# A state-space layer and an MLP on one core: table sums moved between GpSimd, VectorE and TensorE

## The chip, the core and the metric

The kernel runs on one core of a Trainium2 chip. The core has TensorE (PE, matmuls, with its weight loads as PEld), VectorE (DVE), ScalarE (ACT), GpSimd (POOL) and SyncE (SP, which issues the DMAs here). Each runs its own instructions in a fixed order, and they wait for one another by semaphores. The metric is the device time of one execution in microseconds (us), as the median of several runs. Times inside an execution come from one profiled execution, counted from the start of its span.

## What is computed

One layer of a diffusion backbone over 256 latent and 256 context tokens of width 2048: an S5 state-space mixer, a GLU, and a squared-ReLU MLP, each with RMSNorm and modulation by a conditioning vector.

```python
h = modulate(rmsnorm(x, norm_mix_pre), sh1, sc1)        # ctx and latent, own shift and scale
lam_bar = exp(lam * dt); b_bar = ((lam_bar - 1) / lam)[..., None] * b   # 128 groups, 64 states, complex
for direction in range(2):                               # forward and reverse
    st_ctx = s5_scan(u_ctx, lam_bar, b_bar, 0)           # s[t] = lam_bar * s[t-1] + b_bar u[t]
    st_lat = s5_scan(u_lat, lam_bar, b_bar, st_ctx_final)
    y = y + einsum('btgp,ghp->btgh', st_lat, c_mat).real
a, g = split(gelu(y) @ w_glu); y = a * sigmoid(g)
x = x + gt1 * rmsnorm(y, norm_mix_post)
x = x + gt2 * rmsnorm(square(relu(modulate(rmsnorm(x, norm_mlp_pre), sh2, sc2) @ w1)) @ w2, norm_mlp_post)
```

## The kernel before

The 256 time steps are cut into 32 chunks of 8, and the 128 groups into 16 blocks of 8 groups, each block into two half blocks of 4 groups. All of the S5 mixer lies in about the first 420 us.

**Per half block, the input tables (E).** A chunk's input reaches the state through b_bar times powers of lam_bar. The product of two complex numbers is made with three multiplications. GpSimd makes the sums s1e = Qr + Qi (Q are the powers) and s2e = Br + Bi, Br - Bi (`e_sums`, once a block). VectorE makes the three products k = s1e*Br, Qr*s2e, Qi*s2e (`e_op`, 128x512 each), then subtracts the latter two from k into e[1] and e[0] (two more 128x512 instructions, e<-k,e in the profile). PE transposes the eight 128x128 parts of e against the identity (`e_tr`, tile tr), ScalarE copies them to et (`e_ev`). PE also multiplies e with the diagonal blocks cbd of C into a "strip" st (`strip`), from which the table for the within-chunk part comes, over wps and W, and a DMA round trip through DRAM (wd, then eight DMAs into it). With et and the normalised input xz, PE makes the chunk inputs (`v_mm`, tile v), which ScalarE copies (`v_ev`) into the tables ctx and lat.

**Per unit of 4, 6 and 6 blocks, the scan.** VectorE runs over the context chunks in a tree of steps and over the latent chunks one by one, 31 steps of three instructions each (lines 727, 732 and 734, tiles t, ctx, lat), which depend on each other.

**Per block, the output.** `d_sums` on GpSimd makes s1d and s2d from the powers P and from C (loaded as bcc); VectorE makes three products for each half block (`d_op`, tiles dx in a ring of 4 buffers, dy for the last two blocks). ScalarE copies the states out of lat (`sp_copy`, two instructions), GpSimd adds their real and imaginary parts (`sp_sum`), and PE makes y (`out_mm`), followed by Gelu.

Beside this PE multiplies the conditioning vector with its weights (tile ada, from loads raw<-wa and raw<-wk of 1 MB each into three buffers), and GpSimd applies norm and modulation to the input (xz<-xz,rs and xz<-xz,vec). Behind S5 come the GLU (tile gb, PE) and the MLP (tiles m and o, PE), which the change does not touch.

What sets the order: `Plan` takes every task with its engine, an assumed duration, what it depends on, and rings of buffers that it takes and gives back, and lists them engine by engine; each engine then runs its list in that order, whatever the real times. SP's list holds all loads. A table `PR` holds priorities and where the sums run (`sums`, `spsum`). In the profile, line 122 is the helper for all tensor_tensor instructions, and line 125 that for ScalarE's activations, so there one goes by tiles.

Of the kernel before, what the change touches and what calls it, by code (L numbers as in the profile page):

```python
# [116 lines left out]
def _body(ctx, tc, nc, I, O):  # L117
# [111 lines left out]
    with psx:  # L229
# [55 lines left out]
        sk = ew.tile([128, L, 4, H], F32, name="sk")  # L285
        cbd = [ew.tile([128, 8, 2, 32], F32, name=f"cbd{n}") for n in range(2)]
# [116 lines left out]
        for name, cap in (("ada", 1), ("ev", 1), ("bcb", 2), ("bcs", 2), ("bcc", 2), ("s1e", 2), ("s2e", 1), ("sd", 2), ("cbd", 2),  # L403
                          ("k1", 1), ("dd", 1), ("e", 2), ("et", 2), ("tr", 2), ("st", 1), ("v", 1), ("x", 2), ("yv", 1), ("sk", 1), ("W", 1), ("it", 1),
                          ("ctx", 1), ("lat", 2), ("dx", 4), ("sp", 2), ("z", 1), ("t", 1), ("it2", 1)):
            plan.ring(name, [0.0] * cap)
# [7 lines left out]
        PR = dict(ada=4, T=20, st=3, V=1, W=5, om=5, E=0, D=2, D0=8, gate=0, k4=5, gap=1, p=-1, ars=3, g=6, g2=20, evm=10, eg1=6, x1=6, zlo=4, z=8, ada2=0, k4l=4, acc=20, lo=1, hi=5, sums='Pool', spsum='Pool')  # L414
# [35 lines left out]
        pt = [add("ACT", 0.95, lambda d=d, s=s, g=g, l=l: p_copy(d, s, g, l), prio=PR["p"]) for d, s, g in ((Pr, pr, 1.0), (Pn, pi, -1.0)) for l in (True, False)]  # L450
        t = []
# [179 lines left out]
        def strip(b, hf):  # L631
            e = est[b, hf][1]
# [75 lines left out]
        def v_ev(b, hf):  # L708
# [7 lines left out]
            act(cx[:, :, :, gu:gu + 4], pv[:, 0:32])  # L716
            act(lt[:, 1:, :, gu:gu + 4], pv[:, 32:63])
# [41 lines left out]
        def d_op(b, hf, f):  # L759
# [51 lines left out]
        for b in range(NB):  # L811
# [4 lines left out]
            esum = add(PR["sums"], 0.55 if on_v else 1.1, lambda b=b: e_sums(b), ([bcl["b", b]] if b > 1 else []) + gate + (qt if b == 2 else []), prio=1, take=("s1e", "s2e"))  # L816
            cb = add("ACT", 0.6, lambda b=b: c_diag(b), [bcl["s", b]] if b > 1 else [], prio=1, take=("cbd",), give=("bcs",))
            for hf in range(2):
                p = PR["E"]
                o = [add("DVE", 0.6, lambda b=b, h=hf: e_op(b, h, 0), [esum], prio=p, take=("k1", "e"))]  # L820
                for k in (1, 2):
                    o.append(add("DVE", 0.6, lambda b=b, h=hf, k=k: e_op(b, h, k), [(o[-1], 0.0)], prio=p))
                o.append(add("DVE", 0.6, lambda b=b, h=hf: e_op(b, h, 3), [(o[0], 0.13), (o[2], 0.13)], prio=p))
                o.append(add("DVE", 0.6, lambda b=b, h=hf: e_op(b, h, 4), [(o[3], 0.0), (o[1], 0.13)], prio=p, give=("k1",) + (("s1e", "s2e", "bcb") if hf else ())))
                tps, evs = [], []
                for r in range(2):
                    tps.append(add("PE", 0.43, lambda b=b, h=hf, r=r: e_tr(b, h, r), [o[3 + r]] + tps, prio=PR["T"], take=("tr",)))
                    evs.append(add("ACT", 0.48, lambda b=b, h=hf, r=r: e_ev(b, h, r), [tps[r]] + [(x, 0.0) for x in evs], prio=0,
                                   take=("et",) if r == 0 else (), give=("tr",)))
                sm = add("PE", 0.57, lambda b=b, h=hf: strip(b, h), [o[4], cb] + tps, prio=PR["st"], take=("st",), give=("e",) + (("cbd",) if hf else ()))  # L830
# [650 lines left out]
```

## Time and profile before

| | before |
|---|---|
| median of 3 runs | 1312.68 us (1308.35 to 1317.29) |
| profiled execution | 1313.43 us, span 1311.7 us |
| PE busy | 1178.7 us (90%) |
| VectorE busy | 897.1 us (68%) |
| ScalarE busy | 539.4 us (41%) |
| GpSimd busy | 192.5 us (15%) |
| granted TensorE clock, mean | 0.953 |
| HBM traffic | 225 GB/s over the span |

The shares of the span are means over stages with different limits, so they are read stretch by stretch. Busy time is the union of an engine's instructions; on PE, matmuls overlap. The granted clock is the share of TensorE's full speed that it was allowed in a stretch. The DMA share is the mean busy share of the core's 16 DMA engines.

### The profile page before, as it was taken

The numbers are of one execution on the slowest core, as the hardware profiler recorded it, in microseconds if no ns is written. First come the engines' busy times: TensorE is split into PE (matmuls) and PEld (weight loads), VectorE is DVE, ScalarE is ACT, GpSimd is POOL, SyncE is SP. The second block draws the span as 40 slices with busy tenths as digits, with TensorE's granted clock in tenths as the row PEclk, the third lists the DMA queues.
The fourth block names the chain that finished last, engine by engine and source line by source line (L and its number), as shares of the span: only waits on it lengthen the run. The fifth ranks groups of instructions, "written<-read, shape, count | busy, mean of one in ns | idle before, by whom it ended". The sixth has DMA issues, their size and how long they took to land.

```text
span 1311.7 us, 22524 instructions
## 1 busy us (share of the span) xinstructions
PE 1178.7 (90%) x9457; PEld 957.2 (73%) x9457; DVE 897.1 (68%) x1200; ACT 539.4 (41%) x731; POOL 192.5 (15%) x200
## 2 busy tenths in 40 slices
PE   4576884696898999989999999999999999999997
PEld 1454553452434688989999999999978888888885
DVE  8999999878878677765555565555655555655555
ACT  5442544242115534574333334333434444444443
POOL 4766344611322000030000000000000000000000
PEclk8588997798899999999999999999999999999998
DMA  7488868989986888816656666566656555555552
GB/s 269 148 213 295 316 245 195 307 307 196 260 227 168 319 346 324 317 66 224 234 219 245 217 220 250 209 242 223 230 189 224 192 193 184 182 185 188 192 192 97
DMA packets 74093, 296.68 MB, mean 226 GB/s; under 512 B 7164, under 2 KB 30588, under 8 KB 48520
## 3 DMA queue, kind: packets, MB, share of 16 engines
q1 hardware_dynamic: 73992, 295.25, 66.3%
q8 instruction: 74, 1.21, 0.4%
q14 instruction: 27, 0.22, 0.1%
HBM read 291.15 MB, written 4.07 MB: 225 GB/s over the span
## 4 chain that ended last, share of the span: by engine, by line
PE 74%; DMA 9%; DVE 5%; SPq 1%; ACT 1%; issue 1%; POOL 0%; DVEq 0%; POOLq 0%; ACTq 0%
PE m L1325 27%; PE o L1358 27%; PE gb L998 9%; DMA raw<-wk 4%; PE gb L991 3%; DMA it<-wd 2%; DMA raw<-wa 2%; DVE e L122 2%; SPq L689 1%; PE ada L484 1%; PE y L800 1%; PE v L706 1%; DMA bcc<-bc 1%; PE m L1247 1%; PE ada L476 1%
## 5 line engine op out<-in xcount | busy, mean ns | idle before, releaser
L122 DVE TENSOR_TENSOR wlo<-raw,whi 128x2048 fp32r<-128x2048 f32 x126 | 288.7, 2291 | 134.7 <-ACT whi L125 134.7
L1325 PE MATMUL m<-h,whi 128*128 128x256 f32 x1984 | 248.2, 283 | 0.0
L125 ACT ACTIVATE whi<-raw 128x2048 fp32r<-128x2048 f32 (+1 forms) x130 | 243.8, 1876 | 1.5 <-PE m L1247 1.5
L1325 PEld LDWEIGHTS m<-h,whi 128*128 128x128 f32 x1984 | 242.5, 192 | 0.0
L1358 PE MATMUL o<-wlo,hh 128*128 128x512 f32 x512 | 160.5, 395 | 0.2 <-DVE wlo L122 0.2
L1358 PE MATMUL o<-whi,hh 128*128 128x512 f32 x512 | 160.6, 395 | 0.0
L1358 PE MATMUL o<-whi,hl 128*128 128x512 f32 x512 | 160.5, 395 | 0.0
L1325 PE MATMUL m<-h,wlo 128*128 128x256 f32 x992 | 129.1, 283 | 0.0
L1325 PEld LDWEIGHTS m<-h,wlo 128*128 128x128 f32 x992 | 123.5, 192 | 0.0
L125 ACT ACTIVATE hh<-hid 128x512 fp32r<-128x512 f32 x64 | 40.5, 633 | 194.5 <-PE o L1358 194.5
L125 ACT ACTIVATE r<-m 128x256 f32<-128x256 f32 x64 | 24.6, 384 | 222.9 <-PE m L1325 221.1
L1358 PEld LDWEIGHTS o<-wlo,hh 128*128 128x128 f32 x512 | 95.9, 187 | 24.1 <-DVE wlo L122 0.6
L1358 PEld LDWEIGHTS o<-whi,hh 128*128 128x128 f32 x512 | 95.8, 187 | 24.2 <-ACT hh L125 0.8
L1358 PEld LDWEIGHTS o<-whi,hl 128*128 128x128 f32 x512 | 96.0, 187 | 23.5
L1297 DVE TENSOR_TENSOR hl<-hid,hh 128x512 fp32r<-128x512 f32 x64 | 44.3, 693 | 88.8 <-ACT hh L125 88.7
L1269 DVE TENSOR_TENSOR hid<-r,m 128x256 f32<-128x256 f32 x64 | 26.9, 421 | 91.9 <-ACT r L125 91.9
L991 PE MATMUL gb<-raw,xz 128*128 128x512 f32 x160 | 76.0, 623 | 2.4 <-DMA raw<-wg 2.3
L623 PE MATMUL tr<-ident,e 128*128 128x128 f32 x256 | 44.7, 315 | 30.9 <-DVE e L122 24.6
L998 PE MATMUL gb<-hi,zs 128*128 128x512 f32 (+1 forms) x288 | 70.1, 357 | 0.0
L484 PE MATMUL ada<-raw,cst 128*32 128x512 f32 x256 | 36.9, 654 | 35.4 <-DMA raw<-wk 35.4
L623 PEld LDWEIGHTS tr<-ident,e 128*128 128x128 f32 x256 | 32.5, 160 | 45.8 <-DVE e L122 21.4
L991 PEld LDWEIGHTS gb<-raw,xz 128*128 128x128 f32 x160 | 30.2, 197 | 46.5 <-issue 40.2
(202 smaller groups left out, 1613.2 us busy)
## 6 DMA issues: line engine op xcount, KB each, us to landing
raw<-w SPq DMA_DIRECT2D x128, 1024.0 KB, 4.8
raw<-wk SPq DMA_DIRECT2D x48, 1024.0 KB, 8.4
raw<-wa SPq DMA_DIRECT2D x32, 1024.0 KB, 7.4
raw<-wg SPq DMA_DIRECT2D x32, 1024.0 KB, 5.2
k<-wk SPq DMA_DIRECT2D x16, 1024.0 KB, 7.3
it<-wd SPq DMA_DIRECT2D x64, 128.0 KB, 6.9
xz<-xs SPq DMA_DIRECT2D x4, 1024.0 KB, 9.1
bcb<-bc SPq DMA_DIRECT2D x16, 128.0 KB, 8.9
```

The costliest lines, as they stand in the source:

```text
L122: eng.tensor_tensor(out=out, in0=a, in1=b, op=op)
L125: A.activation(out=out, in_=in_, func=f, **kw)
L476: PE.matmul(adab["a"][32 * j:32 * j + 32, :n], cst[:, 2 * kt:2 * kt + 32], w[:, e, j], start=(kt == 0), stop=(kt == KT - 1))
L484: PE.matmul(adab["k"][32 * j:32 * j + 32, :], cst[:, 2 * kt:2 * kt + 32], w[:, j * 512:(j + 1) * 512], start=(kt == k0), stop=(kt == KT - ...
L623: PE.transpose(est["ps"][:, gi * 128:(gi + 1) * 128], e[:, r, gi].rearrange("p s h -> p (s h)"), ident)
L689: S.dma_start(it[16 * s:16 * s + 16], wdt[b2][:, :, (7 - s) * H:(7 - s) * H + 128])
L991: PE.matmul(banks[p][nk * t + k], xz[kt // BQ][:, GQ * C + (kt % BQ) * T + t * 128:][:, :128], wt[:, (nk * e + k) * 512:(nk * e + k + 1) * ...
L998: PE.matmul(banks[p][nk * t + k][:, :wd], a, w[:, (nk * e + k) * wd:(nk * e + k + 1) * wd], start=ff, stop=ll)
L1269: V.tensor_tensor(out=hid[:, nt], in0=r, in1=ps, op=ALU.mult)
L1297: V.tensor_tensor(out=hl, in0=hid[:, 2 * i:2 * i + 2], in1=hh.bitcast(F32), op=ALU.subtract)
L1325: PE.matmul(ps, w[a][:, kt], (h2h, h2l)[b][:, kt], start=a == b == kt == 0, stop=a == 1 and kt == KT - 1)
L1358: PE.matmul(banks[nh][2 * t + k], w[2 + x][:, e, zz], w[y][:, e * 1024 + k * 512:e * 1024 + k * 512 + 512], start=f and n == 0 and e == es ...
```

## The change

The subtractions leave VectorE. k gets the negative sum Qs = -(Qr + Qi), which is made once for all blocks (`q_sum`), so that each element of the table is minus (k + e). PE adds the two: for each 128x128 part, a transpose of k starts the sum in PSUM and a transpose of e accumulates on it. The strip's matmuls take k and e one after the other as well. The minus sign is taken out in ScalarE's copies behind PE (scale -1.0). All small sums (s2e, s1d, s2d, sp) now run on VectorE. The ring of k goes from 1 to 2 buffers, that of dx from 4 to 3, and s1e is gone. Since the tasks and their assumed durations change, the planner orders the first 420 us anew.

```diff
+        def q_sum(b0, b1):
+            a, b, o = (w[:, b0:b1].rearrange("p b t g -> p (b t g)") for w in (Qr, Qi, Qs))
+            V.scalar_tensor_tensor(out=o, in0=a, scalar=-1.0, in1=b, op0=ALU.mult, op1=ALU.subtract)
+        q_sum(0, 2)
...
-                          ("k1", 1), ("dd", 1), ("e", 2), ("et", 2), ("tr", 2), ("st", 1), ("v", 1), ("x", 2), ("yv", 1), ("sk", 1), ("W", 1), ("it", 1),
-                          ("ctx", 1), ("lat", 2), ("dx", 4), ("sp", 2), ("z", 1), ("t", 1), ("it2", 1)):
+                          ("k1", 2), ("dd", 1), ("e", 2), ("et", 2), ("tr", 2), ("st", 1), ("v", 1), ("x", 2), ("yv", 1), ("sk", 1), ("W", 1), ("it", 1),
+                          ("ctx", 1), ("lat", 2), ("dx", 3), ("sp", 2), ("z", 1), ("t", 1), ("it2", 1)):
...
-        PR = dict(ada=4, T=20, ..., sums='Pool', spsum='Pool')
+        PR = dict(ada=4, T=20, ..., sums='DVE', spsum='DVE')
...
+        qs = add("DVE", 1.05, lambda: q_sum(2, NB), qt, prio=0)
...
         def e_sums(b):
             Bv = bct.pop(("b", b))
-            s1 = ew.tile([128, L, 8], F32, tag="s1e", bufs=2, name="s1e")
-            tt(SE, s1, Qr[:, b], Qi[:, b], ALU.add)
...
         def e_op(b, hf, k):
-            if k < 3:
-                o, p, c = ((k1, s1, Bv[:, 0]), (e[:, 1], Qr[:, b], s2[:, 0]), (e[:, 0], Qi[:, b], s2[:, 1]))[k]
-                tt(V, o, p[...]..., c[...]..., ALU.mult)
-            else:
-                tt(V, e[:, k - 3], k1, e[:, k - 3], ALU.subtract)
+            o, p, c = ((k1, Qs[:, b], Bv[:, 0]), (e[:, 0], Qi[:, b], s2[:, 1]), (e[:, 1], Qr[:, b], s2[:, 0]))[k]
+            tt(V, o, p[...]..., c[...]..., ALU.mult)
...
             for gi in range(4):
-                PE.transpose(est["ps"][:, gi * 128:(gi + 1) * 128], e[:, r, gi].rearrange("p s h -> p (s h)"), ident)
+                for n, w in enumerate((k1[:, gi], e[:, r, gi])):
+                    PE.matmul(est["ps"][:, gi * 128:(gi + 1) * 128], w.rearrange("p s h -> p (s h)"), ident, is_transpose=True, start=(n == 0), stop=(n == 1))
...
-            for r in range(2):
+            for n, (r, w) in enumerate(((0, k1), (1, k1), (0, e[:, 0]), (1, e[:, 1]))):
                 for j in range(4):
-                    PE.matmul(st[32 * j:32 * j + 32, :128], cbd[b % 2][:, hf * 4 + j, r], e[:, r, j].rearrange("p s h -> p (s h)"),
-                              start=(r == 0), stop=(r == 1))
+                    PE.matmul(st[32 * j:32 * j + 32, :128], cbd[b % 2][:, hf * 4 + j, r], w[:, j].rearrange("p s h -> p (s h)"),
+                              start=(n == 0), stop=(n == 3))
...
-            act(sk[:, :, lp], est.pop(("st", b, hf))[:, :128].rearrange("p (s h) -> p s h", h=H))
+            act(sk[:, :, lp], est.pop(("st", b, hf))[:, :128].rearrange("p (s h) -> p s h", h=H), scale=-1.0)
...
-            act(cx[:, :, :, gu:gu + 4], pv[:, 0:32])
-            act(lt[:, 1:, :, gu:gu + 4], pv[:, 32:63])
+            act(cx[:, :, :, gu:gu + 4], pv[:, 0:32], scale=-1.0)
+            act(lt[:, 1:, :, gu:gu + 4], pv[:, 32:63], scale=-1.0)
```

The order on VectorE, first in the first unit's latent scan (t and lat are the scan's), before:

```order
L122 TENSOR_TENSOR k_1509<-s1e,bcb 128x512
L732 TENSOR_TENSOR lat<-lat,t 128x64
L122 TENSOR_TENSOR e<-Qr,s2e 128x512
L734 TENSOR_TENSOR lat<-lat,t 128x64
L122 TENSOR_TENSOR e<-Qi,s2e 128x512
L727 TENSOR_TENSOR t<-ARS,lat 128x128
L122 TENSOR_TENSOR e<-k_1509,e 128x512
L732 TENSOR_TENSOR lat<-lat,t 128x64
L122 TENSOR_TENSOR e<-k_1509,e 128x512
L734 TENSOR_TENSOR lat<-lat,t 128x64
```

and with the change, in the same scan:

```order
L122 TENSOR_TENSOR k_1955<-Qs,bcb 128x512
L738 TENSOR_TENSOR lat<-lat,t 128x64
L122 TENSOR_TENSOR e<-Qi,s2e 128x512
L740 TENSOR_TENSOR lat<-lat,t 128x64
L122 TENSOR_TENSOR e<-Qr,s2e 128x512
L733 TENSOR_TENSOR t<-ARS,lat 128x128
L518 TENSOR_TENSOR r_2002<-vp,m_65 128x32 x4
L738 TENSOR_TENSOR lat<-lat,t 128x64
L122 TENSOR_TENSOR s2e<-bcb 128x128 x2
```

A half block's five VectorE instructions become three, and the next block's two s2e sums stand among them, which read bcb, a load.

On PE the work of one half block (cbd_146 is the buffer of C's diagonal blocks), before:

```order
L623 MATMUL tr<-ident,e 128x128 x8
L636 MATMUL st<-e,cbd_146 32x128 x8
L706 MATMUL v<-xz_75,et 64x64 x16
L649 MATMUL wps<-ident,sk 64x128 x8
L476 MATMUL ada<-raw,cst 32x256 x8
```

and with the change (the last two pairs of the half block's eight, and what follows):

```order
L629 MATMUL tr<-ident,k_1682 128x128
L629 MATMUL tr<-ident,e 128x128
L629 MATMUL tr<-ident,k_1682 128x128
L629 MATMUL tr<-ident,e 128x128
L642 MATMUL st<-k_1682,cbd_146 32x128 x8
L642 MATMUL st<-e,cbd_146 32x128 x8
L485 MATMUL ada<-raw,cst 32x256 x8
L712 MATMUL v<-xz_76,et 64x64 x16
```

Eight transposes become sixteen, in pairs of k and e, and the strip's eight matmuls become sixteen; v stays.

On VectorE behind the last unit's scan, with the change (before, the rows behind the last lat are the dx products alone, and the sp sums stand on GpSimd):

```order
L740 TENSOR_TENSOR lat<-lat,t 128x96
L122 TENSOR_TENSOR sp<-sp 128x256 x2
L122 TENSOR_TENSOR dx<-s1d,bcc 128x512
L122 TENSOR_TENSOR dx<-Pn,s2d 128x512
L122 TENSOR_TENSOR dx<-Pr,s2d 128x512
L122 TENSOR_TENSOR sp<-sp 128x256
L122 TENSOR_TENSOR dx<-s1d,bcc 128x512
L122 TENSOR_TENSOR dx<-Pn,s2d 128x512
L122 TENSOR_TENSOR dx<-Pr,s2d 128x512
L122 TENSOR_TENSOR s1d<-Pr,Pn 128x64
L122 TENSOR_TENSOR s2d<-bcc 128x128 x2
```

The sums that stood on GpSimd now stand between the products, in VectorE's one order.

## Rows read from the trace of the kernel before

**Rows 1.** Busy time by stretch: stretch, its length, engines, granted clock, DMA share, GB/s.

```profile
20.00:205.00 185.00, 124.80 (x2073) 88.26 (x2077) 176.45 (x351) 73.37 (x175) 98.47 (x99) 0.81 0.70 238
205.00:436.00 231.00, 180.40 (x2041) 96.37 (x2033) 189.92 (x409) 80.64 (x131) 70.33 (x66) 0.91 0.89 241
436.00:560.00 124.00, 124.00 (x633) 103.65 (x632) 94.86 (x80) 56.01 (x77) 0.00 (x0) 1.00 0.85 329
...
586.00:1311.00 725.00, 716.83 (x4520) 644.49 (x4518) 403.82 (x292) 295.45 (x270) 0.95 (x1) 1.00 0.57 206
```

**Rows 2.** Chain that ended last, shares by line, 20 to 205, then 205 to 436.

```profile
by line: DMA raw<-wa 12.0%; DVE e L122 10.4%; PE ada L476 5.2%; DVE lat L734 3.6%; PE v L706 3.6%; DVE t L727 3.4%; DVE lat L732 2.8%; PE tr L623 2.6%; issue 2.3%; DVE k L122 2.0%; PE wps L649 1.7%; PE st L636 1.5%; DVE t L730 1.1%; DVE ctx
...
by line: DMA raw<-wk 20.1%; PE gb L991 14.9%; DMA it<-wd 10.8%; SPq L689 7.3%; PE ada L484 6.7%; PE y L800 5.9%; DMA bcc<-bc 5.5%; DMA raw<-wg 3.7%; DVE dy L122 3.3%; PE v L706 2.7%; PE y L798 2.6%; issue 2.5%; ACT sp L125 2.5%; PE tr L623 
```

**Rows 3.** VectorE by form, 20 to 205: busy us, mean ns; idle before, releasers.

```profile
L122 DVE TENSOR_TENSOR e<-k,e 128x512 f32<-128x512 f32 x46 | 35.1, 771 | 0.1
L122 DVE TENSOR_TENSOR e<-Qr,s2e 128x512 f32<-128x512 f32 x24 | 20.1, 838 | 0.8 <-PE st L636 0.8
L122 DVE TENSOR_TENSOR e<-Qi,s2e 128x512 f32<-128x512 f32 x23 | 20.0, 871 | 0.0
L122 DVE TENSOR_TENSOR k<-s1e,bcb 128x512 f32<-128x512 f32 x24 | 18.9, 789 | 1.2 <-POOL s1e L122 1.2
L727 DVE TENSOR_TENSOR t<-ARS,lat 128x128 f32<-128x128 f32 x29 | 13.2, 455 | 0.3
L734 DVE TENSOR_TENSOR lat<-lat,t 128x64 f32<-128x64 f32 x28 | 11.0, 393 | 0.3
L732 DVE TENSOR_TENSOR lat<-lat,t 128x64 f32<-128x64 f32 x29 | 9.3, 319 | 0.2
```

**Rows 4.** VectorE in order of time: start us, us, instruction.

```profile
59.83 0.29 DVE L433 TENSOR_TENSOR sq<-ARS 128x128 f32<-128x128 f32 x1
60.03 0.28 DVE L434 SCALAR_TENSOR_TENSOR ARS<-ARS 128x128 f32<-128x128 f32 x1
...
61.12 0.68 DVE L122 TENSOR_TENSOR e<-Qr,s2e 128x512 f32<-128x512 f32 x1
61.72 0.68 DVE L122 TENSOR_TENSOR e<-Qi,s2e 128x512 f32<-128x512 f32 x1
...
70.12 1.35 DVE L434 SCALAR_TENSOR_TENSOR ARS<-ARS 128x128 f32<-128x128 f32 x1
...
205.67 0.22 DVE L734 TENSOR_TENSOR lat<-lat,t 128x64 f32<-128x64 f32 x1
```

**Rows 5.** GpSimd in order of time, at the same place.

```profile
68.74 2.57 POOL L122 TENSOR_TENSOR xz<-xz,rs 128x512 f32<-128x512 f32 x2
```

**Rows 6.** GpSimd by form, 20 to 205: the norm and modulation of the input.

```profile
L122 POOL TENSOR_TENSOR xz<-xz,vec 128x512 f32<-128x512 f32 x28 | 38.7, 1391 | 29.1 <-DVE vec L522 28.0
L122 POOL TENSOR_TENSOR xz<-xz,rs 128x512 f32<-128x512 f32 x16 | 23.3, 1484 | 1.0 <-DVE rs L398 1.0
```

**Rows 7.** PE in order of time, two places; a strip matmul has two records.

```profile
129.32 1.09 PE L623 MATMUL tr<-ident,e 128*128 128x128 f32 x4 [0.38 <-DVE e L122]
...
169.57 1.09 PE L623 MATMUL tr<-ident,e 128*128 128x128 f32 x8
170.59 0.65 PE L636 MATMUL st<-e,cbd 128*32 128x128 f32 x16
171.05 1.05 PE L476 MATMUL ada<-raw,cst 128*32 128x256 f32 x16
```

**Rows 8.** PE's waits, 20 to 205: total us, times, longest.

```profile
PE sr L395 <- DVE sr L392: 10.4, 1, 10.4
```

**Rows 9.** GpSimd by form, 205 to 436.

```profile
L122 POOL TENSOR_TENSOR s2d<-bcc 128x128 f32<-128x128 f32 x24 | 18.3, 782 | 41.5 <-DMA bcc<-bc 34.3 <-DVE lat L732 7.2
```

**Rows 10.** VectorE by form, 205 to 436.

```profile
L122 DVE TENSOR_TENSOR dx<-s1d,bcc 128x512 f32<-128x512 f32 x24 | 17.6, 734 | 20.1 <-PE y L800 17.3 <-DMA bcc<-bc 2.8
```

**Rows 11.** ScalarE in order of time, behind the last scan.

```profile
387.00 4.42 ACT L125 ACTIVATE sp<-lat 64x512 f32<-64x512 f32 x4 [10.99 <-DVE lat L734]
```

More of the change, by code (lines that the diff above doesn't have):

```diff
@@ L285, in _body @@
         sk = ew.tile([128, L, 4, H], F32, name="sk")
+        Qs = ew.tile([128, NB, L, 8], F32, name="Qs")
         cbd = [ew.tile([128, 8, 2, 32], F32, name=f"cbd{n}") for n in range(2)]
@@ L402, in _body @@
         add = plan.add
-        for name, cap in (("ada", 1), ("ev", 1), ("bcb", 2), ("bcs", 2), ("bcc", 2), ("s1e", 2), ("s2e", 1), ("sd", 2), ("cbd", 2),
-                          ("k1", 1), ("dd", 1), ("e", 2), ("et", 2), ("tr", 2), ("st", 1), ("v", 1), ("x", 2), ("yv", 1), ("sk", 1), ("W", 1), ("it", 1),
-                          ("ctx", 1), ("lat", 2), ("dx", 4), ("sp", 2), ("z", 1), ("t", 1), ("it2", 1)):
+        for name, cap in (("ada", 1), ("ev", 1), ("bcb", 2), ("bcs", 2), ("bcc", 2), ("s2e", 1), ("sd", 2), ("cbd", 2),
+                          ("k1", 2), ("dd", 1), ("e", 2), ("et", 2), ("tr", 2), ("st", 1), ("v", 1), ("x", 2), ("yv", 1), ("sk", 1), ("W", 1), ("it", 1),
+                          ("ctx", 1), ("lat", 2), ("dx", 3), ("sp", 2), ("z", 1), ("t", 1), ("it2", 1)):
             plan.ring(name, [0.0] * cap)
@@ L412, in dve @@
             return (n * 1.04 + 66) / 1e3
-        PR = dict(ada=4, T=20, st=3, V=1, W=5, om=5, E=0, D=2, D0=8, gate=0, k4=5, gap=1, p=-1, ars=3, g=6, g2=20, evm=10, eg1=6, x1=6, zlo=4, z=8, ada2=0, k4l=4, acc=20, lo=1, hi=5, sums='Pool', spsum='Pool')
+        PR = dict(ada=4, T=20, st=3, V=1, W=5, om=5, E=0, D=2, D0=8, gate=0, k4=5, gap=1, p=-1, ars=3, g=6, g2=20, evm=10, eg1=6, x1=6, zlo=4, z=8, ada2=0, k4l=4, acc=20, lo=1, hi=5, sums='DVE', spsum='DVE')
         SE = V if PR["sums"] == "DVE" else GP
@@ L604, in e_op @@
         def e_op(b, hf, k):
-            Bv, s1, s2 = est[b]
+            Bv, s2 = est[b]
             hs = slice(hf * 4, hf * 4 + 4)
@@ L815, in _body @@
             on_v = PR["sums"] == "DVE"
-            esum = add(PR["sums"], 0.55 if on_v else 1.1, lambda b=b: e_sums(b), ([bcl["b", b]] if b > 1 else []) + gate + (qt if b == 2 else []), prio=1, take=("s1e", "s2e"))
+            esum = add(PR["sums"], 0.55 if on_v else 1.1, lambda b=b: e_sums(b), ([bcl["b", b]] if b > 1 else []) + gate + (qt if b == 2 else []), prio=1, take=("s2e",))
             cb = add("ACT", 0.6, lambda b=b: c_diag(b), [bcl["s", b]] if b > 1 else [], prio=1, take=("cbd",), give=("bcs",))
@@ L819, in _body @@
                 p = PR["E"]
[L820 removed]
+                o = [add("DVE", 0.6, lambda b=b, h=hf: e_op(b, h, 0), [esum] + ([qs] if b == 2 else []), prio=p, take=("k1", "e"))]
                 for k in (1, 2):
[L822 to L824 removed]
+                    o.append(add("DVE", 0.6, lambda b=b, h=hf, k=k: e_op(b, h, k), [(o[-1], 0.0)], prio=p, give=("s2e", "bcb") if hf and k == 2 else ()))
                 tps, evs = [], []
                 for r in range(2):
[L827 removed]
+                    tps.append(add("PE", 0.9, lambda b=b, h=hf, r=r: e_tr(b, h, r), [o[1 + r]] + tps, prio=PR["T"], take=("tr",)))
                     evs.append(add("ACT", 0.48, lambda b=b, h=hf, r=r: e_ev(b, h, r), [tps[r]] + [(x, 0.0) for x in evs], prio=0,
                                    take=("et",) if r == 0 else (), give=("tr",)))
[L830 removed]
+                sm = add("PE", 0.8, lambda b=b, h=hf: strip(b, h), [o[2], cb] + tps, prio=PR["st"], take=("st",), give=("k1", "e") + (("cbd",) if hf else ()))
                 lp = 2 * (b % 2) + hf
```

12 lines of the change are left out of this document (6 added, 6 removed).

## The prediction

> **What bounds the kernel now.** I first cut the span into stretches and read each engine's busy time in them [rows 1]. From 436 us on the change touches nothing: PE is busy 124.00 of 124 us in the GLU and 716.83 of 725 us in the MLP, and these stretches move earlier or later as a block. All edits lie before 436 us, and there two stretches differ. In 20 to 205 us, where 24 of the 32 half blocks build their tables, VectorE is busy 176.45 of 185 us and PE 124.80. In 205 to 436 us VectorE is busy 189.92 of 231, PE 180.40, and the DMA share is 0.89. Second, the chain of the work that ended last, for each stretch [rows 2]: up to 205 us it mixes VectorE's e and scan instructions, PE and the raw loads; behind 205 us it is mostly transfers and their queue: raw<-wk 20.1%, it<-wd 10.8%, SP's issues 7.3%, bcc<-bc 5.5%, raw<-wg 3.7%, together 47%. So VectorE time can be turned into kernel time mainly ahead of 205 us. Third, VectorE's instructions by form [rows 3], and what stands beside the slow ones on GpSimd [rows 4, 5].
>
> **VectorE, 20 to 205 us.** Removed: the subtractions k minus e, 46 in this stretch with a mean of 771 ns [rows 3]. A record is about 0.08 us longer than the step to the next instruction (two 128x512 instructions start at 61.12 and 61.72 us, each of 0.68 us [rows 4]), so each costs 0.69 us: 46 x 0.69 = 31.8 us.
> Added: the 24 s2e sums of 128x128. No such sum ran on VectorE; the nearest row is the 128x128 square at 59.83, whose follower starts at 60.03 [rows 4]: 0.20 us. With eight s2d sums of the same size and four s1d sums of half of it at most that price, 36 x 0.20 = 7.2 us. The new table Qs is one instruction of 128 and one of 896 columns; from 0.20 us at 128 and 0.60 at 512 columns the second is 1.0 us: 1.2 us. Sum 8.4 us.
> Moved off GpSimd: its instructions slow VectorE's. The same ARS instruction (L434) takes 0.28 us at 60.03 and 1.35 us at 70.12, where GpSimd works on xz [rows 4, 5]. Against what such instructions take alone (0.68 us at 512 columns, 0.29 at 128, 0.22 at 64 [rows 4]), the means of [rows 3] hold an excess of 46 x 0.091 + 24 x 0.158 + 23 x 0.191 + 24 x 0.109 + 29 x 0.165 + 28 x 0.173 + 29 x 0.099 = 27.5 us. Of GpSimd's 98.47 us in this stretch [rows 1], 62.0 us are the xz instructions, which stay [rows 6]; 36.5 us, 37%, are mostly the small sums. I give them the same share of the excess, 10 us; the bounds are 0 and 27.5.
> The Trainium skill (Perfetto Trace Analysis, Optimizing Scalar/DVE Operations) says both that a saturated VectorE may hand work to GpSimd and that, since the two share an SBUF read port, this might not help. The first half speaks against this change; L434's 0.28 and 1.35 us bear out the second half. By the first half alone the relief would be 0 and the next sum -23.4 us.
> Sum: -31.8 + 8.4 - 10 = -33.4 us (bounds -23.4 and -50.9). VectorE would then need 176.45 - 33.4 = 143 us, with the 8.5 us that it idles now 152 us.
>
> **PE, 20 to 205 us, is late next.** Each half block has eight transposes more. Eight took 1.02 us from their start to the next instruction (169.57 to 170.59), the strip's matmuls 0.46 us (170.59 to 171.05) [rows 7]; both double. 24 x (1.02 + 0.46) = 35.5 us, so PE needs 124.80 + 35.5 = 160.3 us. It also can't work while it waits for the norm's sum at the stretch's start, 10.4 us [rows 8]: 171 us. That is an upper value at today's clock, 0.81 of full in the mean [rows 1]: at 129.32 us four transposes took 1.09 us against eight at 169.57 [rows 7], so a clock that is granted more fully shortens all of it. An accumulating pair of transposes is nowhere in the trace; I price the second like the first, the nearest row. The lower value is VectorE's 152 us. I take 165 us, nearer to PE's because its order is fixed and each transpose still waits for VectorE's products: 185 - 165 = **20 us gained**.
>
> **From 205 to 436 us.** VectorE loses 18 subtractions (64 in all less 46) at 0.69, 12.4 us. It gains 8 s2e, 24 s2d, 12 s1d and 16 sp sums (counted in the code; the s2d also in [rows 9]): 44 x 0.20 = 8.8 us, and 16 x 0.33 (256 columns, a third of the way between 0.20 and 0.60) = 5.3 us: 1.7 us more in sum. It also gets waits. The sp sum stands in VectorE's order right behind a unit's scan, two in a row; ScalarE's copies that feed them took 4.42 us for two blocks at 387.00 us [rows 11]. VectorE stands still in that time, and behind it queue the d products for which PE waits: at most 4.4 us after each of the last two scans. Before, GpSimd stood there, and at 387 us VectorE stood anyway, behind the dx ring, whose waits for PE total 17.3 us [rows 10]. The ring goes from four tiles to three, so VectorE's lead shrinks by one tile, three products or 1.8 us at each such wait. PE has eight half blocks at 1.48 us more, 11.8 us of its 50.6 idle us. Against these stand GpSimd's latencies, which go, and loads that may start earlier. Since the transfers set this stretch, I take 0, with -10 and +16 as bounds (the first: half of the first stretch's gain repeated; the second: two waits of 4.4 us, and 1.8 us at four waits for the ring).
>
> **Sum.** -20 + 0. The profiled execution took 1313.43 us (span 1311.7), the median of the runs is 1312.68, 0.7 us lower. 1313.4 - 20 = 1293.4, rounded to **1294 us**.
>
> **Rivals.**
> *More than that.* PE's clock is granted fully once it idles less, so VectorE's 152 us holds (-33), and the raw loads, whose slots PE frees earlier, bring 10 us of the second stretch: 1313.4 - 43 = 1270. For it: the clock is 0.81 in the first stretch and 0.91 in the second. Against it: 47% of the second chain is transfers and their issue.
> *The gain is swallowed.* PE's 171 us holds, 14 us gained, and the second stretch gives some back because the same bytes (0.89 of the engines' time) have to pass in it: 1300 to 1320, say 1308. For it: [rows 2]. Against it: the loads of the first stretch have room (share 0.70).
> *Slower: VectorE takes over GpSimd's waits.* GpSimd stood 34.3 us behind 205 us for the bcc loads [rows 9]; nothing queued behind it but sums. The same sums now stand in VectorE's one order, so a bcc load that lands late holds the scan, which is on the path. If all of it lands on VectorE: -20 + 34.3 = +14, and with the sp waits +23: 1328 to 1337. It decides as soon as more than 20 us of those waits survive on VectorE (33 us for over 1%). Against it: GpSimd waited early, its sums were needed later, and VectorE itself waited for them only 1.2 us in the first stretch [rows 3].
> *Without effect on VectorE's pace*, because GpSimd's xz work fills the time that the sums leave: then only the relief of 10 us goes, VectorE needs 162 us, PE's 165 stands, and the time is the forecast's. It needs no chance of its own.
>
> **How the numbers follow.** The forecast's case, 1283 to 1303, has 0.48; the larger gain, 1265 to 1283, 0.15; the swallowed gain, 1303 to 1322, 0.21; slower, above 1322, 0.16. One per cent of 1312.7 is 13 us, about what a measurement of this kernel can tell from no change: below 1299.6 is faster, above 1325.8 slower. Of the forecast's case 0.40 lies below 1299.6: faster 0.55. Of the slower case 0.13 lies above 1325.8, and 0.32 remain for within 1%. The range leaves out the lowest 0.05 and the highest 0.14: 1270 to 1323.
>
> **What would show it.** In the profile after: 96 products of k and e and no subtraction, their means nearer to 0.68 us; VectorE's 128x128 sums at about 0.29 us a record; the last half block's k at least 20 us earlier than before; PE's transposes 512 with eight accumulating pairs in about 2 us a half block; the GLU's uninterrupted PE work starting near 416 us where it started at 436. I am wrong if VectorE shows waits for bcb or bcc of more than 20 us, if PE waits for raw loads grow by what VectorE saved, or if accumulating transposes take longer than plain ones.

## The result: 1330.5 us, slower by 1.4%

| | before | after |
|---|---|---|
| median | 1313.72 us (1308.35 to 1317.29) | 1330.54 us (1328.44 to 1330.78) |
| ratio | | 1.0138, 95% interval 1.0108 to 1.0167 |
| profiled execution | 1313.43 us, span 1311.7 us | 1330.38 us, span 1328.5 us |
| start of the last half block's k | 282.6 us | 291.5 us |
| start of the GLU's uninterrupted PE work | 436.0 us | 448.7 us |
| first hp matmul behind the GLU | 564.2 us | 580.4 us |
| VectorE busy, whole span | 897.1 us | 867.8 us |

Four runs each. The forecast was 1294 us, range 1270 to 1323. Of the 16.8 us that the span grew, 12.7 us had come by the GLU's start and another 3.5 us between the GLU's start and the first hp matmul (131.7 us where it took 128.2); only 0.6 us came later.

Busy time by stretch in the kernel after; the columns are those of [rows 1]:

```profile
20.00:205.00 185.00, 141.06 (x2521) 109.01 (x2525) 151.64 (x342) 75.37 (x166) 58.86 (x47) 0.83 0.68 233
205.00:436.00 231.00, 187.81 (x2334) 113.69 (x2327) 175.28 (x441) 74.02 (x132) 11.61 (x7) 0.92 0.85 229
```

VectorE is busy 24.8 us less than before in the first stretch and 14.6 us less in the second, PE 16.3 and 7.4 us more. So the work moved as it was meant to, and yet everything ends later. VectorE by form in the kernel after, 20 to 205 us, columns as in [rows 3]:

```profile
L122 DVE TENSOR_TENSOR e<-Qi,s2e 128x512 f32<-128x512 f32 x21 | 20.0, 951 | 0.0
L122 DVE TENSOR_TENSOR e<-Qr,s2e 128x512 f32<-128x512 f32 x21 | 20.0, 951 | 0.0
L122 DVE TENSOR_TENSOR k<-Qs,bcb 128x512 f32<-128x512 f32 x22 | 19.2, 871 | 14.8 <-PE st L642 14.8
...
L122 DVE TENSOR_TENSOR s2e<-bcb 128x128 f32<-128x128 f32 x22 | 8.3, 418 | 0.1
```

Two things stand here. In the same 185 us there are 21 to 22 half blocks where [rows 3] show 23 to 24, with products that take longer (means of 871 to 951 ns instead of 789 to 871), and VectorE, which waited for almost nothing before, now waits 14.8 us for PE's strip to give back a tile of k. VectorE's largest waits in the kernel after from 205 to 460 us (total us, times, longest):

```profile
DVE s2d L122 <- DMA bcc<-bc: 23.1, 9, 6.2
DVE sp L122 <- ACT sp L125: 14.0, 7, 6.6
DVE dx L122 <- PE y L806: 9.8, 5, 4.3
```

The waits that GpSimd had for bcc [rows 9] are now VectorE's, as the rival of the slower case had it; the waits of the dx ring [rows 10] have become shorter.

### The profile page after: what moved, and what is told of

Same layout as the page of the kernel before. It is cut to its first block, busy times and chain, and to the rows that moved or that the text cites. A ratio compares the mean times of both kernels' runs of the same rounds, so it can differ in the third digit from the quotient of the medians.

```text
span 1328.5 us, 23889 instructions
## 1 busy us (share of the span) xinstructions
PE 1216.6 (92%) x10225; PEld 1000.7 (75%) x10225; DVE 867.8 (65%) x1234; ACT 542.4 (41%) x731; POOL 94.2 (7%) x88
## 4 chain that ended last, share of the span: by engine, by line
PE 79%; DVE 8%; DMA 8%; ACT 2%; issue 1%; SPq 1%; DVEq 0%; ACTq 0%
PE m L1329 27%; PE o L1362 27%; PE gb L1002 9%; PE gb L995 3%; PE tr L629 3%; DMA it<-wd 3%; DMA raw<-wk 2%; PE v L712 2%; DMA raw<-wa 2%; PE st L642 2%; PE ada L485 1%; PE ada L493 1%; DVE e L122 1%; DMA bcc<-bc 1%; PE y L806 1%
## 5 line engine op out<-in xcount | busy, mean ns | idle before, releaser
L629 PE MATMUL tr<-ident,k 128*128 128x128 f32 x256 | 65.4, 294 | 3.1 <-issue 2.1
L629 PE MATMUL tr<-ident,e 128*128 128x128 f32 x256 | 63.2, 286 | 2.7 <-DVE e L122 2.7
L1002 PE MATMUL gb<-hi,zs 128*128 128x512 f32 (+1 forms) x256 | 65.5, 366 | 0.0
L125 ACT ACTIVATE et<-tr 128x512 f32<-128x512 f32 x64 | 37.8, 599 | 66.3 <-PE tr L629 58.9
```

What stands on the lines that cost most here:

```text
L125: A.activation(out=out, in_=in_, func=f, **kw)
L629: PE.matmul(est["ps"][:, gi * 128:(gi + 1) * 128], w.rearrange("p s h -> p (s h)"), ident, is_transpose=True, start=(n == 0), stop=(n == 1))
L1002: PE.matmul(banks[p][nk * t + k][:, :wd], a, w[:, (nk * e + k) * wd:(nk * e + k + 1) * wd], start=ff, stop=ll)
```

## The experiments

Three theories were held against each other. P: PE's added work bounds the tables. W: the sums bring GpSimd's waits into VectorE's order. O: the order that the planner writes anew costs the time. All times below are medians, and differences are taken to runs of the kernel before that were taken together with them on the same chip (medians 1313.1 to 1314.3 us). Each median's own interval is some 2 to 5 us to either side, so a difference of two runs' losses is known to within 3 to 6 us.

### Each part alone, as the planner orders it

**pe_half**: the order of the change, but PE takes e alone.

```diff
-                for n, w in enumerate((k1[:, gi], e[:, r, gi])):
+                for n, w in ((0, e[:, r, gi]),):
...
-            for n, (r, w) in enumerate(((0, k1), (1, k1), (0, e[:, 0]), (1, e[:, 1]))):
+            for n, (r, w) in enumerate(((0, e[:, 0]), (1, e[:, 1]))):
```

> The changed kernel in its own order, but PE transposes e alone and the strip takes e alone: k is made by VectorE and read by nobody, so the tables lack k. Theory P (the added PE work bounds the stretch in which the tables are built): PE loses 32 x 1.48 = 47 us of work there, the GLU's uninterrupted work starts at 436 us or earlier instead of 449, time 1295 to 1315. Theory W (VectorE's new waits for bcc, sp and the strip hold the path): the order and those waits stay, the time stays within 6 us of the changed kernel, 1325 to 1331.

Measured 1322.16 us, ratio 1.0065 (1.0040 to 1.0089), outside both ranges. In this order PE's added work accounts for 8 of the 17 us, and without it the kernel is still slower than before: P is at most half of it.

**pe_only**: the change with the sums left on GpSimd (`sums='Pool', spsum='Pool'`), planned anew.

> The changed kernel with all small sums planned and run on GpSimd again; the PE part of the change alone. Theory P: PE bounds the tables as before, 1322 to 1335. Theory W: VectorE's waits for bcc (23.1 us) and for ScalarE's sp copies (17.0 us) go back to GpSimd, and the time falls to 1313 or below.

Measured 1320.79 us, 1.0067 (1.0040 to 1.0093), close to P's range and far from W's: the PE part is no gain as planned here.

**sums_only**: the kernel before with `sums='DVE', spsum='DVE'`, planned anew.

> The kernel before with the small sums planned and run on VectorE; the other part of the change alone, PE's work as before. Theory P: no loss of its own, 1300 to 1318. Theory W: most of the loss is here, 1322 to 1335.

Measured 1330.36 us, 1.0135 (1.0100 to 1.0169). So the sums alone, with the subtractions still there and planned anew, give the whole loss, though VectorE has no more to do up to the GLU: it is busy 366.8 us from 20 to 455 us (its GLU starts at 454.3), against 366.4 from 20 to 436 us before.

**dsums_gp**: the order of the change, but the s1d, s2d and sp sums are issued to GpSimd.

```diff
-            tt(SE, s1, Pr[:, b], Pn[:, b], ALU.subtract)
+            tt(GP, s1, Pr[:, b], Pn[:, b], ALU.subtract)
```

and the same for s2 and for `sp_sum`.

> The changed kernel in its own order, but the s1d, s2d and sp sums are issued to GpSimd though they are planned for VectorE; the s2e sums stay on VectorE. Theory P: PE still bounds the tables until 310 us, and only what follows gains: 1322 to 1330. Theory W: the 40 us of waits for bcc and sp leave VectorE, 1310 to 1318.

Measured 1332.38 us, 1.0151 (1.0125 to 1.0178): no gain. VectorE's waits of s2d for bcc and of sp go, and its waits of dx for PE (y) grow from 10.5 to 30.2 us: in this order another wait takes the place of the one that went. Neither P nor W explains the four runs together, so theory O was tested next by keeping the old order.

### The same work in the order of before

**sums_old_order**: the planner is told that the sums are GpSimd's, and they are issued to VectorE.

```diff
-        SE = V if PR["sums"] == "DVE" else GP
-        SPE = V if PR["spsum"] == "DVE" else GP
+        SE = SPE = V
```

> The kernel before, its order of every engine kept as planned, and only the 36 + 36 + 16 small sums issued to VectorE where they were issued to GpSimd; the planner still believes that they are GpSimd's, so nothing else is re-ordered. Theory O (the re-planned order costs the time): the sums themselves are harmless, 1305 to 1318, while the same sums with a re-planned order took 1330.4. Theory W (VectorE in order meets the loads' and copies' waits, wherever the sums stand): 1325 to 1336, with waits of s2d for bcc and of sp for ScalarE of more than 20 us together.

Measured 1319.79 us, 1.0058 (1.0035 to 1.0081). Between both theories: the waits that W announced are there (14.5 us of s2d for bcc and 9.2 us of sp behind 205 us), but the sums cost 6.7 us where they stand, and planning them anew costs 10 us more (sums_only).

**pe_old_order**: VectorE's subtractions go, PE transposes and strips each table twice, in the old order.

```diff
-            else:
-                tt(V, e[:, k - 3], k1, e[:, k - 3], ALU.subtract)
...
-                PE.transpose(est["ps"][...], e[:, r, gi]..., ident)
+                for n in range(2):
+                    PE.matmul(est["ps"][...], e[:, r, gi]..., ident, is_transpose=True, start=(n == 0), stop=(n == 1))
...
-            for r in range(2):
+            for n, r in enumerate((0, 0, 1, 1)):
```

> The kernel before in its own order with the subtractions of the tables left out and each transpose and strip matmul of a table done twice (accumulated), so that VectorE and PE do the amounts of work of the PE part of the change, without any re-planning and with the sums on GpSimd. It leaves k out of the tables. Theory O: the saved 0.69 us per subtraction comes through as far as PE lets it, 1290 to 1306. Theory P (PE's added work takes it all): 1312 to 1330, with the last half block's k no earlier than 282 us and PE's waits for e gone.

Measured 1308.83 us, 0.9969 (0.9953 to 0.9984): a gain of 4.3 us, between theory O's range and P's. Much the same work planned anew, with three d tiles (pe_only), is 11.4 us slower, each against its own runs of before.

**all_old_order**: both edits above together.

> Both parts in the order of the kernel before: subtractions left out, transposes and strip matmuls doubled, sums issued to VectorE; k is left out of the tables. This is the amount of work of the change without its re-planned order and without its ring of three d tiles. Theory O: 1288 to 1308, at least 20 us under the changed kernel. Theories P and W: 1322 to 1336, like the changed kernel.

Measured 1318.56 us, 1.0047 (1.0029 to 1.0065), between the theories: 11.4 us under the changed kernel, each against its own runs of before, where theory O wanted 20, and still slower than the kernel before. So the order is a cause, and not the only one.

**nosub_old_order**: only the subtractions go.

```diff
-            else:
-                tt(V, e[:, k - 3], k1, e[:, k - 3], ALU.subtract)
```

> The kernel before in its own order with only the 64 subtractions of the tables left out (k is missing from the tables); PE does what it did before, sums on GpSimd. It prices VectorE's saving alone; with PE's doubled transposes and strip on top, in the same order, the time was 1308.8. Theory P (PE's added 1.48 us a half block eats VectorE's saving): 1285 to 1298. Theory F (the saving was never there to be had, because order, rings and transfers set the pace): 1304 to 1313.

Measured 1299.54 us, 0.9894 (0.9868 to 0.9919): 13.8 us less, 1.5 us above P's range and well under F's. The saving was there, and PE's doubled work takes 9.5 us of it back.

**esums_pe_old**: pe_old_order with the s1e and s2e sums alone on VectorE.

```diff
-            tt(SE, s1, Qr[:, b], Qi[:, b], ALU.add)
+            tt(V, s1, Qr[:, b], Qi[:, b], ALU.add)
```

and the same for the two of s2.

> The PE part in the order of before (subtractions left out, transposes and strip doubled, k missing from the tables: 1308.8) with only the s1e and s2e sums of the tables issued to VectorE; the d sums and sp sums, which wait for late loads and for ScalarE, stay on GpSimd. If only the waiting sums hurt (theory W for d and sp): 1303 to 1310. If the sums hurt by standing on VectorE at all: 1312 to 1319.

Measured 1313.41 us, 1.0000 (0.9981 to 1.0020). VectorE shows no wait of these sums for a load, and still they cost 4.4 us; theory W for d and sp alone falls. The remaining sums (all_old_order) cost 5.3 us.

### The order itself

**plan_lags**: the change with the planner's assumed durations set to the trace's.

```diff
-   ... load_bc(n, b), ..., lag=2.0)
+   ... load_bc(n, b), ..., lag=dict(b=8.0, s=3.0, c=7.0)[n])
...
-            sc = add("ACT", 1.04, lambda b=b: sp_copy(b), ...
+            sc = add("ACT", 2.25, lambda b=b: sp_copy(b), ...
```

and e_tr 1.02, strip 1.0, the it loads' lag 7.0.

> The changed kernel with the planner's numbers set to what the trace shows: bc loads landing 8, 3 and 7 us after their issue (2 before), the sp copy 2.25 us (1.04), four transposing pairs 1.02 us (0.9), the strip 1.0 us (0.8), the loads of it 7 us. Theory O: with truer numbers the plan puts waiting instructions later, 1305 to 1318, and VectorE's waits for bcc and sp fall from 40 us to under 20. Theories P and W: no better than the changed kernel, 1325 to 1336.

Measured 1335.13 us, 1.0175 (1.0145 to 1.0205). The time is where P and W had it. VectorE's waits for bcc and sp fell to 17.7 us, as theory O had it, and others took their place (24.4 us of k for PE's strip, 18.8 us of dx for PE). The first hp matmul starts at 576.5 us even so, 3.9 us earlier than in the kernel after (580.4); what the kernel loses it loses behind that, where PE waits 7.6 us for ScalarE's h in front of the MLP (0.6 us in the kernel after). Truer numbers gave a shorter way to hp, but no better order as a whole.

**ring3**: the kernel before with `("dx", 3)` and `bufs=3`, planned anew.

> The kernel before, re-planned, with one part of the change alone: a ring of three d tiles where there were four. Theory O (any re-planning of the tuned order costs some 10 us): 1318 to 1328, also with the transition behind the GLU at 131 us instead of 128. If the ring costs only its own waits: 1313 to 1318, and the dx waits for PE rise from 17 us by at most 8.

Measured 1325.16 us, 1.0081 (1.0046 to 1.0117), in theory O's range; the dx waits for PE behind 205 us rise from 17.3 to 29.7 us, by more than the 8 of the other case. The last k starts at 293.3 us instead of 282.6, the GLU at 448.5. The time from the GLU's start to the first hp matmul stays at 128.2 us, against theory O. Ring and order still had to be told apart.

**replan4**: not one instruction changed, two numbers of the planner are.

```diff
-                    tps.append(add("PE", 0.43, lambda b=b, h=hf, r=r: e_tr(b, h, r), ...
+                    tps.append(add("PE", 0.51, lambda b=b, h=hf, r=r: e_tr(b, h, r), ...
...
-                sm = add("PE", 0.57, lambda b=b, h=hf: strip(b, h), ...
+                sm = add("PE", 0.46, lambda b=b, h=hf: strip(b, h), ...
```

> The kernel before, ring of four, every instruction the same; only two numbers of the planner are changed (four transposes 0.51 us instead of 0.43, the strip 0.46 instead of 0.57, which is what the trace shows), so that it writes another order. Theory R: 1310 to 1317. Theory O: 1318 to 1328.

Measured 1320.88 us, 1.0048 (1.0027 to 1.0070): another order of the same instructions costs 6.6 us, in the lower part of theory O's range and clearly not nothing. The last k starts at 286.4 us, the GLU at 440.6.

**ring4_new**: the change, planned anew, with four d tiles.

```diff
-        Qs = ew.tile([128, NB, L, 8], F32, name="Qs")
+        Qs = Qi
...
-                 ... tag="k1e", bufs=2, name="k1"),
+                 ... tag="k1e", bufs=1, name="k1"),
...
-                for n, w in enumerate((k1[:, gi], e[:, r, gi])):
+                for n, w in enumerate((e[:, r, gi], e[:, r, gi])):
...
-                  ("ctx", 1), ("lat", 2), ("dx", 3), ...
+                  ("ctx", 1), ("lat", 2), ("dx", 4), ...
```

and the tile's `bufs=4`; the strip takes e twice as well.

> The changed kernel re-planned with a ring of four d tiles instead of three. To make room, PE takes the e product twice instead of k and e, and the sum of Qr and Qi is written over Qi; the tables are therefore not the reference's, the number and size of the instructions are those of the change. Theory R (the smaller ring is what costs the last 12 us): 1314 to 1322, dx waits for PE under 8 us. Theory O (any order planned anew costs about 10 us against the one of before): 1325 to 1335.

Measured 1327.35 us, 1.0105 (1.0071 to 1.0138), in theory O's range, although the dx waits behind 205 us are down to 3.3 us. The GLU starts at 446.2 us (448.7 with three tiles, 440.8 in all_old_order). The run changes one thing more: PE no longer reads k, so that VectorE's waits to get a tile of k back from PE's strip (15.4 us in the kernel after) are gone, and 7.1 us of e's stand there. So of the step from the old order to the new, the ring and k's waits together have 3 to 4 us, which the intervals don't fully separate from nothing, and the order most of the rest.

**sc2_last**: the change with the second adaLN scale's two instructions behind the x1 work in VectorE's order.

```diff
-        sct = add("DVE", 0.3, sc2_fin, [t], prio=0, give=("ada",))
+        sct_after = t
...
+        sct = add("DVE", 0.3, sc2_fin, [sct_after] + r2, prio=0, give=("ada",))
```

> The changed kernel with the two vector instructions of the second adaLN scale (which wait for a late PE result) placed behind the x1 work in VectorE's order, as the kernel before has them in effect. Theory O for the transition: the 3.5 us behind the GLU come back, 1326 to 1328, and the time from the GLU's first matmul to the first hp matmul is 128.2 us instead of 131.7. If that order is not the cause: 1330 to 1331 and 131.7 us.

Measured 1336.54 us, 1.0172 (1.0150 to 1.0194), worse by 6. PE in order of time behind the GLU, in all_old_order, in the kernel after and in sc2_last:

```profile
568.96 10.20 PE L1172 MATMUL hp<-dg,xn 128*128 128x128 f32 x64 [2.09 <-DVE dg L1156]
```

```profile
580.39 10.23 PE L1178 MATMUL hp<-dg,xn 128*128 128x128 f32 x64 [5.38 <-DVE dg L1162]
```

```profile
579.32 9.27 PE L1178 MATMUL hp<-dg,xn 128*128 128x128 f32 x64 [4.30 <-DVE dg L1162]
588.34 0.36 PE L1252 MATMUL m<-h,whi 128*128 128x256 f32 x1
588.54 0.28 PE L1252 MATMUL m<-h,wlo 128*128 128x256 f32 x1
594.58 0.58 PE L1252 MATMUL m<-h,whi 128*128 128x256 f32 x1 [5.75 <-ACT h L125]
594.95 0.42 PE L1252 MATMUL m<-h,wlo 128*128 128x256 f32 x1
```

The wait for dg shortens by 1.1 us, and PE then stands 5.75 us in front of the MLP for ScalarE's h, which reads the postponed scale and starts at 585.05 us instead of 581.66. The profile names PE's hp, not the scale, as what h waited for last, so that the scale is the reason is not shown. What else delays dg (the wait is 2.09 us in the old order) was not isolated; the scale's place is a third of it.

### A kernel from what paid

**pe_part_whole**: the PE part in the old order, whole: k and e accumulated on PE, Qr kept negative, the sums on GpSimd.

```diff
-            tt(SE, s1, Qr[:, b], Qi[:, b], ALU.add)
+            tt(SE, s1, Qi[:, b], Qr[:, b], ALU.subtract)
...
-            tt(SE, s2[:, 1], Bv[:, 0], Bv[:, 1], ALU.subtract)
+            tt(SE, Bv[:, 1], Bv[:, 1], Bv[:, 0], ALU.subtract)
...
+                for n, w in enumerate((k1[:, gi], e[:, r, gi])):
+                    PE.matmul(est["ps"][...], w..., ident, is_transpose=True, start=(n == 0), stop=(n == 1))
```

> The PE part of the change in the order of before, now with the tables of the reference: Qr is kept with its sign turned, PE accumulates the transposes and strip matmuls of k and e, k has two tiles, and the room for the second comes from writing the differences of B and C over one half of their own tiles; the sums stay on GpSimd, four d tiles, no planning anew. From the chain of runs: -13.8 for the subtractions and +9.3 for PE, 1305 to 1312, under both kernels. If the later release of the B and C tiles holds up their loads: 1314 to 1322.

Measured 1309.81 us over 12 runs, 0.9976 (0.9958 to 0.9994): faster than the kernel before by a quarter of one per cent, with an interval that only just leaves out no change, and faster than the kernel after. The step run pe_old_order, in which PE took e twice, had shown 4.3 us; this one has 3.5.

## Why the prediction was wrong, point by point

The runs form a chain in which one thing changes at a time, except in its last row, which takes three together (median less that of its own runs of before):

| kernel | to before, us | step, us |
|---|---|---|
| subtractions gone (nosub_old_order) | -13.8 | -13.8 |
| PE's work doubled (pe_old_order) | -4.3 | +9.5 |
| s1e, s2e on VectorE (esums_pe_old) | +0.1 | +4.4 |
| s1d, s2d, sp on VectorE (all_old_order) | +5.4 | +5.3 |
| new order, ring of three, k in PE's work (the change) | +16.8 | +11.4 |

The steps depend on what already stands: the same sums cost 6.7 us with the subtractions in place (sums_old_order) and 9.7 us without them. In the forecast's terms, the first stretch's gain of 20 us was 4.3 us where the order stood still; the sums, which had 2.8 us to their credit there (10 less 7.2) and nothing against them in the second stretch, cost 9.7; and the order, which had no term, brought 11.4 together with the ring.

**The step that failed first: "PE is late next", and the stretch taken from the larger of two totals.** The forecast put 20 to 205 us at 165 us, between VectorE's 152 and PE's 171, which counted one wait of PE (10.4 us) as unavoidable. In the old order, with PE's and VectorE's work changed as forecast, the stretch shrank by 3.5 us: the 24th half block's k starts at 200.0 us instead of 203.5. Busy time of 20 to 205 us in pe_old_order:

```profile
20.00:205.00 185.00, 145.52 (x2637) 117.50 (x2641) 153.12 (x314) 74.88 (x176) 88.25 (x101) 0.88 0.73 243
```

VectorE lost 23 us of work and PE gained 21 us; neither is full. What fills the rest are waits in both directions, VectorE's and then PE's in the same kernel and stretch:

```profile
DVE r L509 <- PE vp L497: 10.2, 5, 4.4
DVE e L122 <- PE st L635: 8.4, 4, 3.4
DVE vec L521 <- PE vp L513: 3.4, 4, 1.2
DVE t L729 <- ACT ctx L125: 2.8, 1, 2.8
...
PE tr L622 <- DVE e L122: 14.4, 6, 5.1
PE sr L395 <- DVE sr L392: 10.4, 1, 10.4
PE v L705 <- ACT lat L125: 4.2, 2, 2.4
```

VectorE's waits in this stretch were 6.3 us before and are 28.6 us here. The two engines hand work to each other in two fixed lists. Only 8.4 us of VectorE's waits are those of a ring (e, until the strip has read it); 13.6 us are r and vec, small instructions for the input's modulation, which wait for PE's vp in the same list of PE. So what VectorE saves turns into its waits for PE, while PE still waits 14.4 us for e. With the subtractions gone and PE unchanged (nosub_old_order) the 24th k came 9.95 us earlier, for the 31.8 us that the forecast took off VectorE, and VectorE's waits rose to 22.2 us. The price of 0.69 us a subtraction was not the error; the larger of two totals, as a length, was.

**PE's price was right.** One half block in pe_old_order, sixteen transposes and then the doubled strip (start, us):

```profile
177.07 1.97 PE L622 MATMUL tr<-ident,e 128*128 128x128 f32 x16
178.97 1.08 PE L635 MATMUL st<-e,cbd 128*32 128x128 f32 x32
```

1.90 us from start to start, against 2 x 1.02 in [rows 7]: accumulating pairs cost what plain ones do. The granted clock of the stretch rose from 0.81 to 0.88, as the rival of the larger gain assumed, and the stretch shrank by 3.5 us all the same.

**The relief of 10 us was about 4.** By the prediction's own reckoning (a form's mean less what it takes alone, times its count) the excess of k, e and the latent scan is 26.5 us in pe_old_order and 22.8 us in all_old_order, where all sums have left GpSimd. What the sums add and what they relieve cancel in VectorE's busy time, 153.12 us in the one and 152.85 us in the other, where the forecast had 2.8 us less. It also left out where the sums stand. GpSimd and then VectorE in order of time in esums_pe_old:

```profile
31.85 20.10 POOL L122 TENSOR_TENSOR xz<-xz,rs 128x512 f32<-128x512 f32 x14 [3.69 <-DVE s1e L122]
```

```profile
40.72 1.31 DVE L438 COPY ARS<-ARS 128x128 f32<-128x128 f32 x1
41.95 1.30 DVE L439 TENSOR_SCALAR ARS<-ARS 128x128 f32<-128x128 f32 x1
43.18 1.77 DVE L122 TENSOR_TENSOR k<-s1e,bcb 128x512 f32<-128x512 f32 x1
44.87 1.74 DVE L122 TENSOR_TENSOR e<-Qr,s2e 128x512 f32<-128x512 f32 x1
46.53 1.74 DVE L122 TENSOR_TENSOR e<-Qi,s2e 128x512 f32<-128x512 f32 x1
48.20 1.36 DVE L432 TENSOR_TENSOR sq<-ARS 128x128 f32<-128x128 f32 x1
```

GpSimd in pe_old_order at the same place:

```profile
31.87 6.19 POOL L122 TENSOR_TENSOR xz<-xz,rs 128x512 f32<-128x512 f32 x4 [0.98 <-DVE rs L398]
38.02 0.32 POOL L122 TENSOR_TENSOR s1e<-Qr,Qi 128x64 f32<-128x64 f32 x1
40.49 1.28 POOL L122 TENSOR_TENSOR s2e<-bcb 128x128 f32<-128x128 f32 x2 [2.16 <-issue]
41.74 13.14 POOL L122 TENSOR_TENSOR xz<-xz,rs 128x512 f32<-128x512 f32 x9
```

Before, GpSimd's sums and their waits broke up its run of xz instructions, and VectorE worked at full pace in the gap, on the second half block's products. Without them xz runs 14 times in a row, VectorE beside it takes 1.67 us a product instead of 0.60, and the sums themselves, two blocks' until the fourth k, take 4.6 us there (31.69 to 33.26 and 53.85 to 56.89 us). Starts in us:

| run | 2nd k | 4th k | 5th k | 7th k | 24th k | last k | GLU |
|---|---|---|---|---|---|---|---|
| pe_old_order | 38.5 | 56.7 | 67.9 | 80.6 | 200.0 | 275.4 | 434.8 |
| esums_pe_old | 43.2 | 61.8 | 68.8 | 85.4 | 204.6 | 283.1 | 439.0 |
| all_old_order | 43.2 | 60.6 | 68.0 | 83.3 | 201.3 | 280.0 | 440.8 |

At the fifth k VectorE has made up 4.3 of the 5.2 us. PE has not, and VectorE then waits for it. PE and VectorE in esums_pe_old, then in pe_old_order:

```profile
73.00 1.15 PE L705 MATMUL v<-xz,et 128*64 128x64 f32 x32
76.54 0.42 DVE L509 TENSOR_TENSOR r<-vp,m 128x16 f32<-128x16 f32 x4 [2.71 <-PE vp L497]
```

```profile
68.34 1.15 PE L705 MATMUL v<-xz,et 128*64 128x64 f32 x32 [1.77 <-ACT lat L125]
71.88 0.42 DVE L509 TENSOR_TENSOR r<-vp,m 128x16 f32<-128x16 f32 x4 [0.27 <-PE vp L497]
```

PE is 4.7 us late here, the seventh k is 4.8 us late, and 4.2 us are left at the GLU's start. That this is the price of the s1e and s2e sums is read from the two traces and not shown: no run moved the xz instructions, and in all_old_order, with most of the same early delay, the 24th k is only 1.3 us late. The Trainium skill (SBUF — State Buffer, SBUF: two separate sides) calls the port that VectorE and GpSimd share an exclusive lock, on which the loser waits for the other's whole instruction. The trace agrees: beside xz an instruction of 128 columns and one of 512 lose the same 1.1 us.

**205 to 436 us, taken as 0.** In the old order the s1d, s2d and sp sums cost 5.3 us, all of it behind the tables: in the profiled executions the last k comes 3.1 us earlier than in esums_pe_old and the GLU 1.8 us later. VectorE's waits from 205 to 436 us in all_old_order:

```profile
DVE s2d L122 <- DMA bcc<-bc: 17.4, 6, 4.4
DVE sp L122 <- ACT sp L125: 12.8, 12, 2.2
...
DVE dx L122 <- PE y L798: 3.9, 2, 3.6
```

The mechanism of the slower rival is there (30.2 us of waits), and its rule, that more than 20 us of them decide the case, did not hold: in the old order they go with 5.3 us. Against them stand 20.8 us of dx waits in pe_old_order that fall to 3.9 us. VectorE would have stood behind the dx ring, as the prediction said of 387 us; the sums made it stand earlier. The price is what the two leave over. The rival's 1328 to 1337 us holds the measured time by luck, since the larger part of the loss has another cause.

**What the prediction had no term for: the order planned anew.** The sum was made as if all instructions stayed in the order of before. But planning anew cost 6.6 us with no instruction changed (replan4), and 10.0 us for the same sums (sums_only over sums_old_order). With the ring of three as well it was 11.9 us (ring3) and 11.4 (the change over all_old_order); what the ring has of these two was not separated. The new order of the change puts the first unit's latent scan earlier (its end is at 183.2 us, 209.1 before) and the last tables later; the last table's v copy into ctx ends at 310.1 us instead of 291.4 (all_old_order), and the third unit's scan, which needs it, starts then, at 310.2 us instead of 304.5. A further 3.5 us come behind the GLU. Which single choice of the planner is worth how much stays open: sc2_last and plan_lags, which tried some of them, made it worse.

Of the prediction's signs, the count of the products, the sums at 0.29 us where GpSimd is quiet (s2d, mean 286 ns in the kernel after) and PE's 2 us came; the products' means did not come nearer to 0.68 us but rose, the last k was 8.9 us later instead of 20 earlier, and VectorE's waits for bcc of 23.1 us were the announced sign of an error. PE's waits for the raw<-wk loads did not grow (34.8 us before and 14.0 after, from 205 to 436 us).

## What to carry to other kernels

Where a planner or a pool size writes the order, an edit brings a new order along; price that by planning the unchanged kernel anew with a harmless number or two altered (here 6.6 us, a third of the 19 us looked for), and try the edit in the old order first. When two engines hand work to each other in fixed lists, time saved on one is worth what the waits in both directions leave of it (here 13.8 of some 44 us of subtractions), not the larger of two totals. Small work on a slow, otherwise waiting engine may also be what keeps that engine out of a fast one's way for a while; that was read from traces here, not tested.

## What the runs showed of the hardware

GpSimd's interference is a price per VectorE instruction, not per element: beside a run of xz instructions a 128x128 copy steps on after 1.23 us (40.72 to 41.95) instead of 0.14 (55.79 to 55.93 in pe_old_order), a 128x512 product after 1.69 us (43.18 to 44.87) instead of 0.60, so each loses 1.1 us. The reverse can be larger: one s1e sum of 64 columns on GpSimd took 14.41 us in the kernel before, while VectorE worked without a gap, and 0.32 us in a quieter place (the s1e at 38.02 us, above):

```profile
224.12 14.41 POOL L122 TENSOR_TENSOR s1e<-Qr,Qi 128x64 f32<-128x64 f32 x1
```

In sc2_last the 5.75 us for which PE stood before the MLP cost more than themselves. Behind the wait the granted clock of 594 to 598 us is 0.50, the lower of its two levels (1.2 GHz of 2.4), where it was 1.00 in the kernel after, and the matmuls of m step on every 0.21 us instead of 0.12; they are back at 0.12 from 600.4 us on. The 26 matmuls between took 5.7 us instead of some 3.1. The granted clock of 590 to 640 us is 0.93, where it was 1.00 in the kernel after. PE's busy time is the first number behind the length:

```profile
590.00:640.00 50.00, 45.42 (x357) 45.43 (x358) 23.62 (x26) 24.24 (x39) 9.72 (x14) 0.93 0.41 145
```
